# First layer of a two-layer decoder step: back rotation inside the output matmul, gelu as one ScalarE function, features kept in (channel, group) order

## The chip, the cores and the metric

The kernel runs on one core of a Trainium2 chip. The metric is the device time of one execution in microseconds (us); lower is better. A core has a matrix engine (PE, with its weight loads shown apart as PEld), a vector engine (DVE), an activation engine (ACT), a general engine (POOL) and a queue engine (SP) that issues the DMA transfers. Each engine works through its own instructions in the order in which they stand; between engines they wait on semaphores.

## The reference, cut to what matters

The model is one step of a decoder trunk: one S5 state-space layer, then one stick-breaking attention layer with a shared K/V. Only the S5 layer is touched. Cut to that:

```python
def _s5_layer(x, h0, ...):                    # x: 1024 prompt rows and 8 x 8 sample rows, 1024 features
    h = _rms_norm(x, g_pre)
    u, z = split(h @ w_in)                    # 1024 columns each
    y, hr, hi = _s5_scan(u, h0, ...)          # 64 groups of 16 channels, 64 complex states each
    y = jax.nn.gelu(y)                        # the tanh form
    y = y * jax.nn.sigmoid(y @ w_glu + b_glu) # the gate
    y = y * jax.nn.silu(z)
    return x + _rms_norm(y @ w_out, g_post), hr, hi

# _s5_scan, for each group: bu = w * (B u);  h[t] = lam * h[t-1] + bu[t]  (complex);
# y = Re(C h) + d_skip * u;  the last h is an output
```

## The kernel before, in words

**Stages.** The kernel norms the input rows and turns them to [feature, token] (`xh`, `xl`: every float32 operand is split into two parts, and a product takes three one-pass matmuls, lines 147 to 149). Then comes the S5 layer's main loop (`for ft in range(KT)`, eight tiles of 128 features, 8 groups of 16 channels each), then the gate (`s5_glu`), the output projection (`s5_out`) and the attention. Tokens are kept as 8 steps of a chunk by W = 136 columns (128 prompt chunks, then 8 samples).

**The projections.** `gemm_u(ft)` and `gemm_z(ft)` make one tile of u or z: three column blocks (408, 408 and 272 columns) times 8 k tiles times three matmuls, 72 in all. The u tile goes to DRAM (`u_d`), the z tile too (`zs_d`). In the loop `gemm_u(ft + 2)` and, from ft = 3, `gemm_z(ft - 3)` stand beside the S5 work; the last three z tiles are asked for after the loop. `weights` loads a tile of weights and splits it: ACT copies the high part (line 140), DVE or (odd z tiles) POOL subtracts to give the low part (line 141).

**The loop, tile's matrices.** For each ft: `wb`, `ep`, `fk`, `kp`, `cs` are built by DVE and POOL (all through the helper at line 205, so that they carry one line; they are told apart by tile name). `ep` is turned by PE (line 336) into `et`; `kp` (line 349) is moved by eight DMAs into the triangular matrix `tg` (line 360); `cs` is spread by four DMAs into `cf` = the cosines and sines (`cof`, `sif`; line 378).

**The loop, units.** The tile's u comes back from DRAM as `ug` with rows (step, channel) by eight DMAs (line 389). The 8 groups then go in three units of 3, 3 and 2 groups. A unit: PE makes the chunk inputs `pg` (line 394); ACT copies the two halves of `pg` crosswise into `tb` (400, 401); DVE and POOL rotate (`ta`, `tb`); DVE scans over the chunks (408); ACT copies the halves of the scanned states crosswise into `ts` (412, 413); POOL multiplies `ts` by the sines, DVE multiplies `ta` by the cosines and adds the two into `hs` (the back rotation), and into `l1` for the last state; PE adds two float32 products into one bank, `fk` with `hs` (425) and `tg` with `ug` (426); ACT evacuates to `yg` (427). After the three units comes gelu over the whole tile: ACT Square (430), DVE (431), ACT Sigmoid (432), DVE multiply. Eight DMAs write it to `y_d` (436).

**After the loop.** `yr` is loaded from `y_d` (452) and split by ACT and DVE (453, 454); the gate's matmuls read it.

**What sets the order.** The order on each engine is made by a scheduler that walks the program by modelled times and priorities: the two blocks under `tc.high_priority(OFA)` are put ahead of the projections, which fill PE between them. A pool with `bufs=n` hands out n buffers under a tag; the n+1st waits for the first's readers.

The lines that the steps below rest on most:

```python
tt(Q, ts[:, :n], ts[:, :n], sif[:, gl], ALU.mult)
tt(V, ta[:, :n], ta[:, :n], cof[:, gl], ALU.mult)
tt(V, hs[:, :n, 1:NC], ta[:, :n, 0 : NC - 1], ts[:, :n, 0 : NC - 1], ALU.add)
tt(V, l1[:, gsl], ta[:, :n, NC - 1], ts[:, :n, NC - 1], ALU.add)
```

(`V` is DVE, `Q` is POOL.) The functions in full, with the line numbers of the profile:

## Time and profile before

| what | value |
|---|---|
| median of 3 runs | 1519.7 us (1519.53 to 1520.04) |
| span of the profiled execution, first to last instruction | 1514.9 us |
| PE busy over the span | 1425.9 us, 94% |
| DVE busy over the span | 967.0 us, 64% |
| ACT busy, POOL busy | 733.8 us, 516.4 us |
| S5 loop with PE's and DVE's share, 105 to 325 us | PE 189.25 of 220 us, DVE 196.88 of 220 us |
| gate, 359 to 442 us | PE 83.00 of 83 us |

The span is 4.8 us below the median of the timed runs; what lies around it is outside the first and the last instruction. Busy time of PE counts pipelined matmuls by modelled ends; in a dense stretch the distance between the starts of two matmuls is their price. "PEclk" is the clock that TensorE was granted, as a share of full speed. An idle time is named with what ended it. The stretch that the change touches lies between 75 and 360 us.

### The profile page before, as it was taken

To read this page: it belongs to the slowest core of one execution; us is meant where nothing else is said; L and a number is where in the kernel's file an instruction comes from. 1 tells how busy PE (TensorE), PEld (TensorE's weight loads), DVE (VectorE), ACT (ScalarE), POOL (GpSimd) and SP (SyncE) were. 2 spreads that over 40 slices of the span, in tenths; PEclk is the share of its full clock that TensorE was granted. 3 is DMA by queue.
4 is the path that set the end of the run, shared out by engine and by line. 5 is a ranking of instruction groups with operands and counts; after the bars stand their busy time and mean duration, and the time that the engine had idled before them with its cause. 6 is when DMAs were issued, how large, how long until landed. Compare 5 with 4: busy or idle time off the path is not lost.

```text
span 1514.9 us, 26931 instructions
## 1 busy us (share of the span) xinstructions
PE 1425.9 (94%) x9648; PEld 1150.4 (76%) x9648; DVE 967.0 (64%) x1535; ACT 733.8 (48%) x1423; POOL 516.4 (34%) x497
## 2 busy tenths in 40 slices
PE   5978888889999989999999999999998999998997
PEld 4968788788986879999988877666565666564766
DVE  6788999857764641110022239897888797889635
ACT  6235454554443433333233337676766666576321
POOL 5565765633421123222211003333333232424200
PEclk9989999999999989999999999999999999999999
DMA  5344755575223343233288673979888786754026
GB/s 193 119 113 114 169 127 131 124 205 208 72 83 112 112 178 139 84 120 107 87 283 288 251 264 113 356 272 324 297 286 277 275 282 233 269 203 138 11 78 214
DMA packets 129415, 276.88 MB, mean 183 GB/s; under 512 B 21505, under 2 KB 66306, under 8 KB 129282
## 3 DMA queue, kind: packets, MB, share of 16 engines
q1 hardware_dynamic: 129282, 275.16, 55.1%
q8 instruction: 76, 1.25, 0.3%
q14 instruction: 57, 0.47, 0.1%
HBM read 225.01 MB, written 39.35 MB: 175 GB/s over the span
## 4 chain that ended last, share of the span: by engine, by line
PE 71%; DVE 12%; issue 4%; DMA 3%; POOL 3%; SPq 2%; ACT 2%; DVEq 0%; POOLq 0%; ACTq 0%
PE psmm L147 6%; PE psmm L149 6%; PE psmm L148 6%; PE psqk L147 6%; PE psqk L148 6%; PE psqk L149 6%; PE psa L946 5%; PE psb L1179 4%; PE psa L987 4%; PE psb L1161 4%; PE psqk L1136 3%; PE psqk L1137 2%; PE psa L147 2%; PE psa L149 2%; PE psa L148 2%
## 5 line engine op out<-in xcount | busy, mean ns | idle before, releaser
L1117 POOL TENSOR_TENSOR ql<-q,qh 128x256 fp32r<-128x256 f32 x64 | 60.9, 952 | 282.2 <-ACT qh L1116 235.4
L1138 ACT ACTIVATE F<-psqk,bp 128x384 f32<-128x384 f32 (+2 forms) x192 | 111.4, 580 | 64.2 <-PE psqk L1137 50.7
L1143 DVE TENSOR_TENSOR_SCAN F<-F,maskb 128x256 f32<-128x256 f32 (+3 forms) x128 | 131.6, 1033 | 13.3 <-ACT F L1138 12.8
L1146 POOL TENSOR_TENSOR S<-S,F 128x255 f32<-128x255 f32 (+3 forms) x64 | 100.8, 1574 | 114.7 <-DVE F L1145 26.5
L1139 ACT ACTIVATE S<-psqk,bp 128x384 f32<-128x384 f32 (+2 forms) x192 | 111.4, 583 | 21.0 <-PE psb L1161 20.9
L1161 PE MATMUL psb<-cst,S 128*128 128x128 f32 x576 | 95.9, 283 | 4.8 <-DVE og L1183 3.8
L1161 PEld LDWEIGHTS psb<-cst,S 128*128 128x128 f32 x576 | 66.6, 142 | 35.6 <-issue 20.1
L1145 DVE TENSOR_TENSOR_SCAN F<-F 128x384 f32<-128x384 f32 (+1 forms) x64 | 79.0, 1234 | 20.1 <-ACT F L1138 19.5
L1179 PE MATMUL psb<-at,vr 128*64 128x256 f32 (+1 forms) x640 | 89.0, 367 | 1.2 <-DVE at L1165 1.2
L946 PE MATMUL psa<-vp,sat 128*32 128x256 f32 x1024 | 86.1, 388 | 0.0
L1136 PE MATMUL psqk<-ks,qh 128*128 128x384 f32 (+2 forms) x192 | 77.2, 402 | 7.0 <-DVE ks L1101 5.2
L987 PE MATMUL psa<-kp,qbd 128*32 128x256 f32 x1024 | 75.5, 389 | 0.3 <-PE psb L1161 0.3
L1179 PEld LDWEIGHTS psb<-at,vr 128*64 128x64 f32 x640 | 46.5, 136 | 36.2 <-issue 10.4
L1165 DVE TENSOR_TENSOR at<-psb,maskb 128x384 f32<-128x384 f32 (+3 forms) x128 | 60.2, 477 | 20.5 <-PE psb L1161 19.9
L147 PE MATMUL psmm<-xh,whi_z 128*128 128x408 f32 (+1 forms) x192 | 65.7, 342 | 4.0 <-ACT ut L275 3.2
L147 PE MATMUL psmm<-x,whi_g 128*128 128x408 f32 (+1 forms) x192 | 66.6, 347 | 1.2 <-DVE gt L736 1.2
L147 PE MATMUL psmm<-xh,whi_u 128*128 128x408 f32 (+1 forms) x192 | 65.9, 343 | 0.2 <-ACT xh L253 0.2
L940 DVE TENSOR_TENSOR_SCAN sF<-sF 128x513 f32<-128x513 f32 x32 | 42.9, 1341 | 36.1 <-ACT sF L937 35.9
L1137 PE MATMUL psqk<-ks,ql 128*128 128x384 f32 (+2 forms) x192 | 65.4, 343 | 0.0
L1136 PEld LDWEIGHTS psqk<-ks,qh 128*128 128x128 f32 x192 | 36.8, 192 | 37.6 <-ACT S L1139 12.6
L148 PE MATMUL psmm<-xl,whi_u 128*128 128x408 f32 (+1 forms) x192 | 65.4, 340 | 0.0
L149 PE MATMUL psmm<-xh,wlo_u 128*128 128x408 f32 (+1 forms) x192 | 65.2, 339 | 0.0
(451 smaller groups left out, 4326.4 us busy)
## 6 DMA issues: line engine op xcount, KB each, us to landing
kp<-cache_kT SPq DMA_DIRECT2D x128, 512.0 KB, 5.8
vp<-cache_v SPq DMA_DIRECT2D x128, 512.0 KB, 5.3
cf<-cs SPq DMA_DIRECT2D x32, 256.0 KB, 4.1
q<-q_d SPq DMA_DIRECT2D x128, 64.0 KB, 4.1
u_d<-ut SPq DMA_DIRECT2D x8, 544.0 KB, 2.8
ug<-u_d SPq DMA_DIRECT2D x64, 68.0 KB, 3.1
y_d<-gt SPq DMA_DIRECT2D x64, 68.0 KB, 2.2
zs_d<-zt SPq DMA_DIRECT2D x8, 544.0 KB, 4.5
```

The lines of the kernel that those rows point to most:

```text
L147: nc.tensor.matmul(ps, sh, mh, start=(k == 0), stop=False)
L148: nc.tensor.matmul(ps, sh, ml, start=False, stop=False)
L149: nc.tensor.matmul(ps, sl, mh, start=False, stop=(k == n - 1))
L946: self.nc.tensor.matmul(po[32 * r : 32 * r + 32, 0:256], a[:, 32 * r : 32 * r + 32], rhs[:, r * 256 : (r + 1) * 256], start=start, stop=stop)
L987: nc.tensor.matmul(ps[32 * r : 32 * r + 32, half * 256 : half * 256 + 256], self.qbd[:, 2 * r + e, s, :], kt[:, :, 2 * r + e, :], start=(e ...
L1136: nc.tensor.matmul(ps[:, :m], qh[:, w], ks[:, c0 : c0 + m], start=True, stop=False)
L1138: nc.scalar.activation(F[:, c0 : c0 + m], ps[:, :m], AF.Sigmoid, bias=bp[:, 1, h : h + 1], scale=-0.125)
L1139: nc.scalar.activation(S[:, c0 : c0 + m], ps[:, :m], AF.Sigmoid, bias=bp[:, 0, h : h + 1], scale=0.125)
L1143: V.tensor_tensor_scan(fr, fr, self.maskb[:, 512 - m : 512][:, ::-1], 1.0, ALU.mult, ALU.max)
L1146: (Q if i % 2 else V).tensor_tensor(S[:, 0 : n - 1], S[:, 0 : n - 1], F[:, 1:n], op=ALU.mult)
L1161: nc.tensor.transpose(ps[:, j * 128 : (j + 1) * 128], S[:, (j0 + j) * 128 : (j0 + j + 1) * 128], self.ident)
L1179: nc.tensor.matmul(po[hs, o:256], self.vr[pi][:, j, hs], ats[hh][j // 4][:, j % 4, o:256], start=(j == 0), stop=(j == nj - 1))
```

## The change

It does these things, all in the S5 layer:

- The back rotation is no longer added up on DVE: DVE writes `ta * cos` straight into `hs`, POOL writes `ta * sin` into `tb`, and PE applies both to the output with two products, `fk` with `hs` and a new matrix `fs` (the halves of `fk` exchanged, one negated, by two ACT copies a tile) with `tb`. So three float32 matmuls a group in place of two; the two ACT copies into `ts` are gone. The `tg` product stands first.
- The last states are collected in `last` by small ACT copies, and rotated once after the loop.
- gelu is one ACT function (`Gelu_apprx_tanh`) that reads PSUM, once a unit; `yg`, Square, Sigmoid and the two DVE instructions are gone. Each unit's result is stored by itself.
- The channels of a u, z and y tile are kept in (channel, group) order: the weight columns are permuted while they are split (`by_channel`: the raw tile is read with a step of 16 elements), and the rows of `w_glu`, `b_glu` and `w_out` are permuted as they are loaded. `u_d` and `y_d` are laid out as [step, channel, group, column]: u is written in pieces of 136 columns and `ug` read by one DMA instead of eight; y is written by three DMAs a tile instead of eight and `yr` read in pieces of 136 columns.
- `dsk` (the skip term) has a tile of its own, and POOL masks it. `cf` is laid out by group.
- `weights` runs at a higher priority.

```diff
+def by_channel(ap):
+    return ap.rearrange("p k (g c) -> p k c g", c=GC)
 def split_w(nc, pool, raw, tag, shape, eng=None, bufs=2):
-    nc.scalar.activation(hi, raw, AF.Copy)
-    (eng or nc.vector).tensor_tensor(lo, raw, hi, op=ALU.subtract)
+    h, l = hi, lo
+    if len(raw.shape) > len(shape):
+        h, l = (x.rearrange("p k (c g) -> p k c g", c=GC) for x in (hi, lo))
+    nc.scalar.activation(h, raw, AF.Copy)
+    (eng or nc.vector).tensor_tensor(l, raw, h, op=ALU.subtract)
...
-        u_d = dram.tile([KT, 128, NTOK], F32, name="u_d")
-        y_d = dram.tile([KT, 128, NTOK], F32, name="y_d")
+        u_d = dram.tile([KT, L, GC, 8, W], F32, name="u_d")
+        y_d = dram.tile([KT, L, GC, 8, W], F32, name="y_d")
...
-                tt(V, sb[:16, 4], sb[:16, 4], bc(ident[:16, 0:16], 1, 8), ALU.mult)
+                tt(Q, dsk, dsk, bc(ident[:16, 0:16], 1, 8), ALU.mult)
...
+                fs = tp.tile([128, 8, L, GC], F32, name=f"fs{ft}", tag="fs")
+                nc.scalar.activation(fs[0:64], fk[64:128, :, 1:, :], AF.Copy)
+                nc.scalar.activation(fs[64:128], fk[0:64, :, 1:, :], AF.Copy, scale=-1.0)
...
-                for t in range(L):
-                    nc.sync.dma_start(ug[t * GC : (t + 1) * GC], usrc[t])
+                nc.sync.dma_start(ug, u_d[ft].rearrange("t c g n -> (t c) g n"))
...
-                    nc.scalar.activation(ts[0:64, :n], ta[64:128, :n], AF.Copy, scale=-1.0)
-                    nc.scalar.activation(ts[64:128, :n], ta[0:64, :n], AF.Copy)
+                    nc.scalar.activation(last[:, 0, gsl], ta[:, :n, NC - 1], AF.Copy)
-                    tt(Q, ts[:, :n], ts[:, :n], sif[:, gl], ALU.mult)
-                    tt(V, ta[:, :n], ta[:, :n], cof[:, gl], ALU.mult)
-                    tt(V, hs[:, :n, 1:NC], ta[:, :n, 0 : NC - 1], ts[:, :n, 0 : NC - 1], ALU.add)
-                    tt(V, l1[:, gsl], ta[:, :n, NC - 1], ts[:, :n, NC - 1], ALU.add)
+                    tt(Q, tb[:, :n, 0 : NC - 1], ta[:, :n, 0 : NC - 1], sif[:, gl, 0 : NC - 1], ALU.mult)
+                    tt(V, hs[:, :n, 1:NC], ta[:, :n, 0 : NC - 1], cof[:, gl, 0 : NC - 1], ALU.mult)
-                        nc.tensor.matmul(o, fk[:, g, 1:, :]..., hs[:, i, :], start=True, stop=False)
-                        nc.tensor.matmul(o, tg[:, g, :], ug[:, g, :], start=False, stop=True)
-                    nc.scalar.activation(yg[:, g0 : g0 + n, :], py..., AF.Copy)
+                        nc.tensor.matmul(py[:, o : o + W], tg[:, g, :], ug[:, g, :], start=True, stop=False)
+                        nc.tensor.matmul(py[:, o + 1 : o + W], fk[:, g, 1:, :]..., hs[:, i, 1:], start=False, stop=False)
+                        nc.tensor.matmul(py[:, o + 1 : o + NC], fs[:, g]..., tb[:, i, 0 : NC - 1], start=False, stop=True)
+                    nc.scalar.activation(gt[:, :n], py..., AF.Gelu_apprx_tanh)
+                    nc.sync.dma_start(ydst[:, gl], gt[:, :n])
-                nc.scalar.activation(gt, yg, AF.Square, scale=math.sqrt(0.044715))
-                V.scalar_tensor_tensor(gt, gt, 1.0, yg, op0=ALU.add, op1=ALU.mult)
-                nc.scalar.activation(gt, gt, AF.Sigmoid, scale=2.0 * math.sqrt(2.0 / math.pi))
-                tt(V, gt, gt, yg, ALU.mult)
-                for t in range(L):
-                    nc.sync.dma_start(ydst[t], gt[t * GC : (t + 1) * GC])
```

The order of the instructions moves with it. Two places matter below. The first is DVE around one unit of the loop (names: `ta` the rotated inputs and states, `tb` and `ts` their other halves, `l` the last states, `psb` the bank of line 394). Before:

```order
L205 TENSOR_TENSOR ta_0_1494<-ta_0_1494,cf_1389 128x384
L205 TENSOR_TENSOR ep_1958<-pk,wb_1949 128x1024
L205 TENSOR_TENSOR ta_3_1525<-psb_1521,cf_1389 128x384
L205 TENSOR_TENSOR sst<-psb_1521,pk 128x24
L205 TENSOR_TENSOR hs_775<-ta_0_1494,ts_0_1505 128x3x127
L205 TENSOR_TENSOR l_783<-ta_0_1494,ts_0_1505 128x3
L205 TENSOR_TENSOR ep_1958<-ep_1958,tm_1959 128x1024
L205 TENSOR_TENSOR ta_3_1525<-ta_3_1525,tb_3_1526 128x384
```

The same place in the changed kernel:

```order
L214 TENSOR_TENSOR ta_0_1465<-ta_0_1465,tb_0_1466 128x384
L214 TENSOR_TENSOR fk_1583<-pk,sb_1552 128x1152
L424 SCALAR_TENSOR_TENSOR ta_0_1465<-rho,ta_0_1465 128x128 x3
L214 TENSOR_TENSOR fk_1583<-fk_1583,tn_1584 128x1152
L214 TENSOR_TENSOR hs_775<-ta_0_1465,cf_1367 128x3x127
L214 TENSOR_TENSOR cs_1614<-cs_1614,m_1616 128x4x128
L214 TENSOR_TENSOR ta_3_1497<-psb_1493,cf_1367 128x384
L214 TENSOR_TENSOR sst<-psb_1493,pk 128x24
```

The sum into `hs` and the one into `l` are gone; `hs` now follows its scans and stands ahead of the next unit's first rotation, which before was put between the product and the sum. The second place is PE at the end of the loop: the last unit's products, and what stands behind them. Before:

```order
L425 MATMUL psa_3085<-hs_777,fk_2955 128x136
L426 MATMUL psa_3085<-ug_2997,tg_780 128x136
L147 MATMUL psmm_3374<-xh_90,whi_z_3343 128x408
L148 MATMUL psmm_3374<-xl_93,whi_z_3343 128x408
L149 MATMUL psmm_3374<-xh_90,wlo_z_3344 128x408
```

And in the changed kernel:

```order
L437 MATMUL psa_2991<-ug_2911,tg_779 128x136
L438 MATMUL psa_2991<-hs_776,fk_2865 128x135
L441 MATMUL psa_2991<-tb_6_2981,fs_2870 128x127
L156 MATMUL psmm_3011<-xl_92,whi_z_3006 128x408
L157 MATMUL psmm_3011<-xh_89,wlo_z_3007 128x408
L155 MATMUL psmm_3011<-xh_89,whi_z_3006 128x408
```

Before, 108 matmuls of z (one and a half tiles) stand between the last unit's products and the first matmul of the gate; in the changed kernel it is 287 (four tiles, but for one matmul). PE changes between the projections and the loop's float32 work 75 times before and 111 times after, counted from the first transposes of line 336 to the gate.

## Rows read from the trace of the kernel before

**Rows 1.** Windows: stretch, length, busy us (instructions) by engine, PEclk, DMA share, GB/s.

```profile
core 0: us, PE busy (x) PEld busy (x) DVE busy (x) ACT busy (x) POOL busy (x), PEclk, DMA share, GB/s
105.00:325.00 220.00, 189.25 (x1214) 174.73 (x1215) 196.88 (x305) 110.02 (x214) 138.40 (x109) 0.95 0.56 135
325.00:359.00 34.00, 30.56 (x185) 29.61 (x185) 18.06 (x13) 16.96 (x21) 5.99 (x2) 1.00 0.87 294
359.00:442.00 83.00, 83.00 (x504) 82.97 (x503) 63.95 (x59) 35.88 (x64) 38.33 (x16) 1.00 0.20 66
```

**Rows 2.** Waits, 105 to 325 us: engine, line, what ended it, total us, times, longest.

```profile
PE psa L425 <- DVE hs L205: 8.7, 9, 2.0
PE psb L394 <- DVE sst L205: 8.2, 4, 4.6
```

**Rows 3.** Groups by shape, 105 to 325 us: busy us, mean ns, idle before.

```profile
L205 DVE TENSOR_TENSOR hs<-ta,ts 128x381 f32<-128x381 f32 x15 | 15.7, 1049 | 1.2 <-POOL ts L205 1.1
L205 DVE TENSOR_TENSOR hs<-ta,ts 128x254 f32<-128x254 f32 x8 | 8.3, 1040 | 0.8 <-POOL ts L205 0.8
L205 DVE TENSOR_TENSOR l<-ta,ts 128x3 f32<-128x3 f32 x16 | 10.8, 673 | 0.0
L205 DVE TENSOR_TENSOR l<-ta,ts 128x2 f32<-128x2 f32 x8 | 5.6, 706 | 0.0
L431 DVE SCALAR_TENSOR_TENSOR gt<-gt,yg 128x1088 f32<-128x1088 f32 x7 | 9.7, 1391 | 0.0
L205 DVE TENSOR_TENSOR gt<-gt,yg 128x1088 f32<-128x1088 f32 x7 | 9.1, 1302 | 0.0
L205 DVE TENSOR_TENSOR sb<-sb,cst 16x128 f32<-16x128 f32 x6 | 3.3, 544 | 0.0
```

**Rows 4.** By tile, 105 to 325 us: count, shortest/median/longest ns, first and last start.

```profile
L205 DVE TENSOR_TENSOR hs<-ta,ts x23: 410/844/2717, 114.9 to 323.7; 128x381 f32<-128x381 f32 x15, 128x254 f32<-128x254 f32 x8
L205 DVE TENSOR_TENSOR l<-ta,ts x24: 144/156/2322, 104.8 to 324.0; 128x3 f32<-128x3 f32 x16, 128x2 f32<-128x2 f32 x8
L431 DVE SCALAR_TENSOR_TENSOR gt<-gt,yg x7: 1275/1279/1631, 134.2 to 311.4; 128x1088 f32<-128x1088 f32 x7
L205 POOL TENSOR_TENSOR tm<-pk,wb x6: 2858/3133/4922, 113.5 to 264.9; 128x1024 f32<-128x1024 f32 x6
```

**Rows 5.** Timeline of PE: start us, length us, group.

```profile
292.46 0.39 PE L426 MATMUL psa<-ug,tg 128*128 128x136 f32 x2
292.69 0.40 PE L425 MATMUL psa<-hs,fk 128*128 128x136 f32 x2
294.48 0.46 PE L149 MATMUL psmm<-xh,wlo_z 128*128 128x408 f32 x1
294.77 0.35 PE L147 MATMUL psmm<-xh,whi_z 128*128 128x408 f32 x1
```

**Rows 6.** Timeline of PE in z tiles, 12 and 16 matmuls apart, and the gate's first.

```profile
336.69 0.35 PE L147 MATMUL psmm<-xh,whi_z 128*128 128x408 f32 x1
338.91 0.34 PE L147 MATMUL psmm<-xh,whi_z 128*128 128x408 f32 x1
...
288.72 0.29 PE L148 MATMUL psmm<-xl,whi_z 128*128 128x272 f32 x1
290.74 0.29 PE L149 MATMUL psmm<-xh,wlo_z 128*128 128x272 f32 x1
...
342.49 0.35 PE L147 MATMUL psmm<-yh,whi_g 128*128 128x408 f32 x1
```

**Rows 7.** Windows, the gate's weights alone: busy us of PE, PEld, DVE, ACT.

```profile
342.49:359.00 16.51, 12.57 (x49) 8.62 (x50) 1.22 (x1) 1.04 (x1) 1.00 0.87 318
```

**Rows 8.** Groups by shape: attention's output written with a step; evacuation and split without.

```profile
L665 ACT ACTIVATE qt<-psqk 128x384 f32<-128x384 f32 x8 | 7.5, 940 | 30.0 <-PE psqk L149 30.0
L275 ACT ACTIVATE ut<-psmm 128x408 f32<-128x408 f32 x16 | 8.1, 509 | 23.7 <-PE psmm L149 17.5 <-issue 6.1
L141 DVE TENSOR_TENSOR wlo_z<-wraw_z,whi_z 128x1024 fp32r<-128x1024 f32 x4 | 4.8, 1208 | 0.0
```

More of the change, by code (lines that the diff above doesn't have):

```diff
@@ L215, in weights @@
         def weights(which, ft):
-            wraw = wp.tile([128, KT, 128], F32, name=f"wraw_{which}{ft}", tag="wraw", bufs=1)
-            nc.sync.dma_start(wraw, io["a_win"][ft + (KT if which == "z" else 0)])
-            return split_w(nc, wp, wraw, f"{which}{ft}", [128, KT, 128], Q if which == "z" and ft % 2 else V)
+            with tc.high_priority(2 * OFA):
+                wraw = wp.tile([128, KT, 128], F32, name=f"wraw_{which}{ft}", tag="wraw", bufs=1)
+                nc.sync.dma_start(wraw, io["a_win"][ft + (KT if which == "z" else 0)])
+                return split_w(nc, wp, by_channel(wraw), f"{which}{ft}", [128, KT, 128], Q if which == "z" and ft % 2 else V)
         gpre = start.tile([128, D], F32, name="gpre")
@@ L296, in s5_layer @@
             hs = tp.tile([128, 3, W], F32, name=f"hs{i}")
-            Q.memset(hs, 0.0)
             h_t.append(hs)
+        last = par.tile([128, 4, G], F32, name="last")
         tgs = [tp.tile([128, 8, 128], F32, name=f"tg{i}") for i in range(2)]
@@ L386, in s5_layer @@
                 ug = work.tile([128, 8, W], F32, name=f"ug{ft}", tag="ug")
-                usrc = u_d[ft].rearrange("(g c) (t n) -> t c g n", c=GC, t=L)
-                for t in range(L):
-                    nc.sync.dma_start(ug[t * GC : (t + 1) * GC], usrc[t])
-                yg = work.tile([128, 8, W], F32, name=f"yg{ft}", tag="yg", bufs=1)
+                nc.sync.dma_start(ug, u_d[ft].rearrange("t c g n -> (t c) g n"))
+                ydst = y_d[ft].rearrange("t c g n -> (t c) g n")
                 for g0, n in ((0, 3), (3, 3), (6, 2)):
@@ L439, in s5_layer @@
         nc.sync.dma_start(gains, io["b_gains"])
+        nc.scalar.activation(last[0:64, 1], last[64:128, 0], AF.Copy, scale=-1.0)
+        nc.scalar.activation(last[64:128, 1], last[0:64, 0], AF.Copy)
+        tt(V, last[:, 2:4], last[:, 0:2], last[:, 2:4], ALU.mult)
+        tt(V, l1, last[:, 2], last[:, 3], ALU.add)
         nc.sync.dma_start(io["o_sp"], l1)
```

54 lines of the change are left out of this document (29 added, 25 removed).

## The prediction, made before the changed kernel ran

> **What bounds the kernel now.** I read the windows first, by stage. In the gate PE is busy 83.00 of 83 us, so whatever ends earlier ahead of it moves the end by as much. In the loop, from 105 us (first output product) to 325 (last), PE is busy 189.25 of 220 us at a clock of 0.95, and DVE 196.88 of 220: PE waits for 30.8 us there, and the engine that has no time left is DVE [rows 1]. Then the waits: the two longest of PE are both ended by DVE, on `hs` (the state that the output product reads) and on `sst`, which stands behind the first rotation of a unit [rows 2]. Then the DVE groups and their spread: `hs` takes 410 ns at the shortest and 2717 at the longest, the tiny `l` 144 and 2322 [rows 3, 4]. So part of DVE's busy time is waiting inside an instruction. From 325 to 359 PE has 3.4 us idle, in the change from z to the gate [rows 1].
>
> I sum against the profiled span of 1514.9 us; the median of the timed runs, 1519.7, is 4.8 above, and I carry a difference over to it unchanged.
>
> **The frame.** Let X be the loop's length in the changed kernel, from its first output product, which I leave at 105 us (the tiles' matrices and the u projections ahead of it are the same). The order puts 287 z matmuls, four tiles, behind the loop, where before it was 108. In a dense stretch 408 columns cost (338.91 - 336.69)/12 = 0.185 us and 272 columns (290.74 - 288.72)/16 = 0.126 [rows 6], so a tile is 48 x 0.185 + 24 x 0.126 = 11.9 us and four are 47.6. The gate then starts at 105 + X + 47.6. Before, 12.6 us of gate work was done by 359 us [rows 7], so it began, as if unbroken, at 346.4. The span changes by X - 193.8. The loop must fall from 220 to 194 us to break even, since 30.3 us of z (47.6 - (342.49 - 325.2) [rows 6]) leave it for behind it.
>
> **What PE gets and loses.** Added: 64 float32 matmuls (`fs` with `tb`, one a group) at 0.23 us, the distance from one product to the next (292.69 - 292.46): 14.7 us. Its neighbour of 136 columns gives the price; 127 columns would be 0.215 at the least, 13.8. Changes between projection and float32 work rise by 36; across one the step was 0.29 in place of 0.185 us (294.77 - 294.48), so 36 x 0.1 = 3.6 us [rows 5]. The loop's PE work now, at full clock, is 189.25 - 0.05 x 220 = 178.2 us. Floor for X: 178.2 + 14.7 + 3.6 - 30.3 = 166.2.
>
> **What DVE loses and gets.** Inside the loop the change takes away the `hs` sums, the `l` sums, two passes of gelu a tile and the `sb` mask: 15.7 + 8.3 + 10.8 + 5.6 + 9.7 + 9.1 + 3.3 = 62.5 us as they ran [rows 3]. Unhindered they are 23 x about 0.5 (`hs` from 410 ns), 24 x 0.15, 7 x 1.275 and 7 x 1.26 [rows 4], with 6 masks at 0.27, taken as half of their mean: some 34 us. The difference, 28 us, is blocked time that another instruction may inherit. The product into `hs` replaces the one into `ta` at the same size and is no term. Added: the low parts of the weights read the raw tile with a step. No row reads so; the nearest is attention's evacuation, which writes with a step of 8 elements: 940 ns for 384 columns against 509 for 408 without, about twice a column [rows 8]. Between nothing and twice, I take twice: six splits on DVE in the loop at +1.2 us (1208 ns now) are +7. So DVE holds 196.9 - 62.5 + 7 = 141 us to 196.9 - 34 + 7 = 170 us. At the share it is busy now (0.895), X is 158 to 190.
>
> **The other engines.** ACT is busy half the loop [rows 1]. Out go the two copies into `ts`, the plain evacuation, Square and Sigmoid; in come gelu from PSUM in the evacuation's place, two copies a tile into `fs`, small copies and splits of twice the price. That about cancels, and it ends no wait of PE worth naming. One more load of an activation table falls into the z tail, under 47.6 us of PE work. POOL keeps its two products a unit, gets the mask (8 small instructions) and slower splits of the odd z tiles: 138 us of 220 become some 145. The new wait is on `fs`: one buffer, so ACT's copies wait for the previous tile's last product, and behind them on ACT stand the evacuations and the copies into `tb`. Two copies of 1024 columns are about 2.5 us by the evacuation's rate [rows 8], once a tile, with z and u matmuls on PE meanwhile: between nothing and 8 x 2.5 = 20 us. I take little, since PE has some 20 projection matmuls (3.7 us) between the tiles' products. SP issues eleven transfers fewer a tile. The pieces of 136 columns that u and y now go through are those in which `ug` and `y_d` moved before; u has a tile of slack and y has the z tail, so I cost the new layout at nothing; uncovered, a slow `yr` would cost its landing, about 5 us.
>
> **A rule to weigh.** `hs` stretches from 410 to 2717 ns and POOL's `tm` from 2858 to 4922 [rows 4]: the two engines hold each other up. The Trainium skill, SBUF — State Buffer, section "SBUF: two separate sides", says that a DVE instruction with two SBUF inputs and a POOL instruction that reads SBUF exclude each other for a whole instruction. By that every removed sum would also free POOL; but as a strict lock it does not fit, since DVE and POOL were busy 335 us in 220 [rows 1], and most of DVE's busy time is of this sort. As far as it holds, it makes a rival (below, "blocked").
>
> **The forecast.** DVE's range (158 to 190) and PE's floor (166) lie close together, so neither engine alone sets X: each will wait for the other at times. PE now loses 42 us to waits and clock over 220. I take X = 183: DVE near its upper end, because POOL's work, which blocks it, stays, and PE with 17 us of waits and slow clock left. That gives 183 - 193.8 = -10.8 us, so 1519.7 - 10.8 = 1508.9, call it 1509. Behind the loop nothing is late: `yr`, the split into `yh` and `yl` and the first `yv` have 47.6 us of z on PE, so the 3.4 us of idle go too (they are in the 346.4).
>
> **The rivals.**
> - *PE is dense.* The blocked time goes with the removed instructions, DVE has slack, and PE runs at its floor with few waits: X = 166 to 175, -28 to -19 us, 1492 to 1501. For it: DVE's lower end is below the floor. Against: the change adds waits of PE on two engines, DVE and POOL, for each group.
> - *Blocked: POOL paces the loop.* The slower side. A unit is a chain: ACT's crosswise copies, POOL's product, DVE's sum and scans, POOL's second product, PE. POOL runs in order, and `tm` (2.9 to 4.9 us) and its like stand between. If the 28 us of blocked time only change their victim and POOL's waits stretch with them, X stays at 197 to 210: +3 to +16 us, 1523 to 1536. It decides from X = 194 on, and only because four z tiles were moved behind the loop: the loop may be 10% faster and the kernel slower. For it: POOL's work does not shrink. Against: POOL is idle for 82 us of the loop.
> - *The step is dear.* If reading with a step costs DVE three times, not twice, six splits in the loop cost 14.5 us rather than 7, and in the gate eight more add 19 us to DVE's 63.95 of 83 [rows 1]: it would be full, and PE would wait. 1517 to 1525. The Trainium skill, SBUF — State Buffer, section "Door 1: The DMA port swizzle", says that accesses beyond a 16-byte line pay a penalty, without a price for DVE; by the row of twice the gate's DVE is at 74 of 83 and hides it.
> - *No gain as described* (gelu slower than the copy that it replaces, a transfer that blocks): 1520 and above. Nothing in the rows speaks for it.
>
> **How the numbers follow.** Forecast 0.42 (1502 to 1516), dense 0.22, blocked 0.20, dear step 0.11, no gain 0.05. A difference under 0.2% (3 us) cannot be told from none here. Faster by more: the forecast's case but for its upper edge, and the dense one: 0.63. Within: the edges of the forecast, of "blocked" and of "dear": 0.13. Slower: the rest, 0.24. The range leaves out the densest end and the worst of "blocked": 1495 to 1528; the forecast's own is 1502 to 1516.
>
> **What would show it.** In the profile after: last output product at about 105 + 183 = 288 us (below 275: dense; above 299: slower than before); DVE busy 141 to 170 us in the loop; no idle of PE between the z tail and the gate; one output product every 0.23 us; the low-part splits at 1.2 us (no price), 2.4 (mine) or 3.6 (dear); gelu from PSUM at about 509 ns for 408 columns. I am wrong if PE's waits move to `tb` from POOL or to `fs` from ACT with totals above 20 us, or if the gate's PE is not full.

## The result and the profile after: 1.1% slower

| | before | changed |
|---|---|---|
| median (lowest to highest) | 1519.9 us (1519.5 to 1523.6) | 1537.2 us (1536.6 to 1539.3) |
| ratio to before, 95% interval | | 1.0109 [1.0094, 1.0123] |
| span of the profiled execution | 1514.9 us | 1534.0 us |
| first matmul of the gate, and from it to the end | 342.5 us (345.9 as if unbroken), 1169.0 us | 365.6 us, 1168.4 us |

The forecast was 1509 us, in a range from 1495 to 1528: the sign is wrong and the time is outside. Counted from the gate's first matmul (before: as if unbroken, since PE waited for 3.4 us in the gate's first 17) the two kernels take the same time within 0.6 us, so the 19.1 us of the span are lost ahead of it.

Windows of the changed kernel: start and end, length, then busy us (instructions) of PE, PEld, DVE, ACT and POOL, the granted clock, the DMA share and GB/s. The stretches are the first 50 us, the loop from its first to its last output product, from there to the gate, the gate's first 84 us, and all up to the gate.

```profile
0.00:50.00 50.00, 29.59 (x160) 27.06 (x161) 34.85 (x85) 28.50 (x49) 22.31 (x74) 1.00 0.43 147
107.45:316.99 209.54, 171.52 (x1183) 159.51 (x1182) 169.85 (x244) 96.19 (x192) 130.63 (x115) 0.95 0.48 127
316.99:365.63 48.64, 47.77 (x289) 47.34 (x288) 18.92 (x11) 22.89 (x27) 10.87 (x4) 1.00 0.81 252
365.63:450.00 84.37, 84.37 (x513) 84.35 (x512) 50.78 (x48) 37.69 (x56) 31.42 (x12) 1.00 0.25 71
0.00:365.63 365.63, 298.51 (x1929) 282.20 (x1930) 268.77 (x426) 167.16 (x297) 202.45 (x232) 0.96 0.51 147
```

The same of the kernel before, for the first 50 us, the loop (again from first to last output product, a little other than in [rows 1]) and all up to the gate:

```profile
0.00:50.00 50.00, 32.62 (x175) 30.07 (x176) 35.60 (x94) 26.35 (x50) 22.30 (x75) 1.00 0.50 169
105.38:325.45 220.07, 189.32 (x1215) 174.90 (x1216) 196.50 (x305) 110.02 (x214) 138.02 (x109) 0.95 0.56 135
0.00:342.49 342.49, 286.72 (x1801) 268.42 (x1801) 284.72 (x490) 162.09 (x305) 202.33 (x225) 0.96 0.55 145
```

The loop is 209.5 us long, 10.5 less than before. But 48.6 us of work stand behind it in place of 17.0, and it begins 2 us later. 194 us were needed to break even. DVE did lose work (169.9 busy of 209.5 in place of 196.5 of 220), and PE did not get it: PE has 38.0 us without work in the loop, before 30.8.

The loop is not one stage. The changed kernel's loop in three parts by DVE's work (its first seven tiles, its wait for the eighth, the eighth), and then the first 176 us of the loop before:

```profile
107.45:281.00 173.55, 136.43 (x948) 124.67 (x947) 158.11 (x221) 80.18 (x164) 120.68 (x105) 0.94 0.50 128
281.00:298.76 17.76, 16.86 (x112) 16.62 (x111) 0.00 (x1) 7.52 (x13) 3.83 (x4) 0.98 0.50 141
298.76:316.99 18.23, 18.23 (x128) 18.22 (x127) 11.74 (x23) 8.48 (x16) 6.12 (x7) 1.00 0.27 99
```

```profile
105.38:281.00 175.62, 148.95 (x952) 136.72 (x953) 162.38 (x245) 86.37 (x169) 117.13 (x91) 0.94 0.57 137
```

PE loses 37.1 of its 38.0 us in the first seven tiles. There DVE is busy 0.91 of the time, hardly less than before (0.92). Behind them DVE has nothing to do for 17.8 us, in which PE finishes the last u tile and works at z.

Waits of PE in the loop (line, what ended it, us in all, times, longest), to be held against [rows 2]:

```profile
PE psa L438 <- DVE hs L214: 20.9, 11, 3.2
PE psm L351 <- DVE ep L214: 5.7, 4, 2.1
PE psb L410 <- DVE sst L214: 4.2, 2, 2.6
PE psa L441 <- POOL tb L214: 1.4, 1, 1.4
```

The wait on `hs` has grown from 8.7 to 20.9 us, though `hs` now takes one DVE instruction less. Where DVE's time went is seen in single instructions, by tile: count, shortest/median/longest ns, first and last start (all of the changed kernel, 103 to 318 us). They answer to [rows 4].

```profile
L214 DVE TENSOR_TENSOR ta<-ta,tb x24: 407/685/3210, 104.7 to 311.9; 128x384 f32<-128x384 f32 x16, 128x256 f32<-128x256 f32 x8
L214 DVE TENSOR_TENSOR ta<-psb,cf x23: 410/543/557, 102.7 to 311.1; 128x384 f32<-128x384 f32 x15, 128x256 f32<-128x256 f32 x8
```

The sum `ta<-ta,tb` was not touched by the change. Its groups in the loop by shape, of the changed kernel and then of the one before (busy us, mean ns of one, idle before it):

```profile
L214 DVE TENSOR_TENSOR ta<-ta,tb 128x384 f32<-128x384 f32 x15 | 21.5, 1435 | 6.1 <-POOL tb L214 6.1
```

```profile
L205 DVE TENSOR_TENSOR ta<-ta,tb 128x384 f32<-128x384 f32 x15 | 10.4, 693 | 0.0
```

Its mean has doubled: it has inherited blocked time that `hs` and `l` had [rows 3, 4]. The product of the same size that reads PSUM on one side is never over 557 ns.

What such an instruction waits for can be seen in the order of time: start us, length us, first on DVE, then on POOL.

```profile
145.76 1.21 DVE L214 TENSOR_TENSOR ep<-pk,wb 128x1024 f32<-128x1024 f32 x1
146.89 2.17 DVE L214 TENSOR_TENSOR ta<-ta,tb 128x256 f32<-128x256 f32 x1
```

```profile
145.91 2.87 POOL L214 TENSOR_TENSOR tm<-pk,wb 128x1024 f32<-128x1024 f32 x1 [0.23 <-DVE wb L214]
```

The sum needs 407 ns where nothing holds it up. Here it begins beside POOL's `tm`, which ends at 148.78, and itself ends 0.28 us later. All 42 DVE instructions of this loop that took over 0.4 us longer than the shortest of their shape have two inputs in SBUF and began while a POOL instruction ran; the time that each took beyond that shortest one is the time to the end of a POOL instruction (that one, or one close behind it), less 0.10 to 0.23 us. Together these excesses are 49.0 us; counted in the same way they are 51.9 us in the loop before (53 instructions). This is called blocked time below. It also stands in POOL's times: `tm` begins 0.15 us after DVE's `ep` and outlasts it by 1.8 us, while the larger product `tn` (128x1152) with no DVE instruction beside it took 2.16 us (at 85.8 us).

Groups up to 480 us: line, engine, what is written from what, shapes and count, busy us and mean ns of one, idle before. They answer to [rows 8]:

```profile
L148 ACT ACTIVATE whi_u<-wraw_u 128x1024 fp32r<-128x1024 f32 x8 | 15.9, 1992 | 7.2 <-PE psmm L156 4.8 <-DMA wraw_u<-a_win 2.4
L149 DVE TENSOR_TENSOR wlo_u<-wraw_u,whi_u 128x1024 fp32r<-128x1024 f32 x8 | 17.8, 2228 | 8.4 <-ACT whi_u L148 8.4
L149 DVE TENSOR_TENSOR wlo_g<-wraw_g,whi_g 128x1024 fp32r<-128x1024 f32 x8 | 15.8, 1977 | 22.9 <-ACT whi_g L148 22.8
L149 POOL TENSOR_TENSOR wlo_z<-wraw_z,whi_z 128x1024 fp32r<-128x1024 f32 x4 | 11.9, 2970 | 4.7 <-ACT whi_z L148 3.4 <-DMA y_d<-gt 1.2
L445 ACT ACTIVATE gt<-psa 128x408 f32<-128x408 f32 x16 | 8.0, 502 | 6.5 <-PE psa L441 5.9 <-DMA u_d<-ut 0.5
```

Reading with a step of 16 elements costs DVE 1977 ns in the gate against 1224 in the kernel before, and ACT 1992 against 1052. The mean of 2228 for `wlo_u` holds blocked time: the shortest took 1883 ns and the longest 3547, before 1195 and 2979. gelu from PSUM takes 502 ns, as long as the plain evacuation did (509).

### The profile page after: what moved, and what is told of

Read it like the earlier page. It is cut to its first block, busy times and chain, and to the rows that moved or that the text cites. A ratio compares the mean times of both kernels' runs of the same rounds, so it can differ in the third digit from the quotient of the medians.

```text
span 1534.0 us, 26976 instructions
## 1 busy us (share of the span) xinstructions
PE 1436.3 (94%) x9776; PEld 1163.3 (76%) x9776; DVE 943.3 (61%) x1465; ACT 739.1 (48%) x1410; POOL 513.6 (33%) x503
## 4 chain that ended last, share of the span: by engine, by line
PE 65%; DVE 12%; issue 9%; POOL 7%; DMA 4%; ACT 2%; SPq 1%; DVEq 0%; POOLq 0%; ACTq 0%
PE psmm L155 5%; PE psmm L157 5%; PE psmm L156 5%; PE psa L960 5%; PE psqk L155 4%; PE psqk L156 4%; PE psqk L157 4%; PE psb L1193 4%; PE psa L1001 4%; PE psb L1175 4%; PE psqk L1150 3%; DMA cf<-cs 2%; DVE ta L214 2%; PE psqk L1151 2%; PE psa L157 2%
## 5 line engine op out<-in xcount | busy, mean ns | idle before, releaser
L1157 DVE TENSOR_TENSOR_SCAN F<-F,maskb 128x256 f32<-128x256 f32 (+3 forms) x128 | 131.3, 1031 | 13.6 <-ACT F L1152 13.1
L1175 PEld LDWEIGHTS psb<-cst,S 128*128 128x128 f32 x576 | 66.4, 142 | 35.6 <-issue 20.5
L1159 DVE TENSOR_TENSOR_SCAN F<-F 128x384 f32<-128x384 f32 (+1 forms) x64 | 79.0, 1234 | 20.3 <-ACT F L1152 19.7
L1193 PEld LDWEIGHTS psb<-at,vr 128*64 128x64 f32 x640 | 46.6, 136 | 36.1 <-issue 10.5
```

Source lines behind the costliest of these rows:

```text
L1157: V.tensor_tensor_scan(fr, fr, self.maskb[:, 512 - m : 512][:, ::-1], 1.0, ALU.mult, ALU.max)
L1175: nc.tensor.transpose(ps[:, j * 128 : (j + 1) * 128], S[:, (j0 + j) * 128 : (j0 + j + 1) * 128], self.ident)
L1193: nc.tensor.matmul(po[hs, o:256], self.vr[pi][:, j, hs], ats[hh][j // 4][:, j % 4, o:256], start=(j == 0), stop=(j == nj - 1))
```

## The experiments

Each ratio is to runs of the kernel before on the same chip; their medians lay between 1519.0 and 1520.2 us. Intervals are about 0.2% to either side, so two kernels less than some 4 us apart are not told apart.

**First question: which part of the change costs?** Theory A: the added PE work is paid in full. Rivals: the step (S), and after the first four runs the priority of the weights (Q) and the layout itself (T).

*Without the step* (after, `e1`; the same for `w_glu`):

```diff
-                return split_w(nc, wp, by_channel(wraw), f"{which}{ft}", [128, KT, 128], Q if which == "z" and ft % 2 else V)
+                return split_w(nc, wp, wraw, f"{which}{ft}", [128, KT, 128], Q if which == "z" and ft % 2 else V)
...
-    a["a_win"] = cols(i["a_w_in"][0])
+    a["a_win"] = mixed(i["a_w_in"][0])
...
```

> The changed kernel, with the columns of w_in and w_glu packed in (channel, group) order ahead of the launch, so that the splits read without a step. Theory A (paid in full): PE waits in the loop for the length of a unit's chain, not for DVE's throughput, so the 64 added products (14.7 us by the prediction) come out at the end nearly whole and the step costs only where it stands on the path, in the first weights: 1531 to 1537 us, loop of some 200 us. Rival S (the step): ACT's splits at 2.0 us in place of 1.05 and DVE's at 2.0 to 2.5 in place of 1.2 hold up the copies into tb and the scans; without the step the loop falls under 194 us and the time to 1515 to 1525.

*Back rotation summed on DVE again* (after, `e2`; `fs` and `last` go, `ts` and `l` come back as in the kernel before):

```diff
-                        nc.tensor.matmul(
-                            py[:, o + 1 : o + NC], fs[:, g].rearrange("p a b -> p (a b)"), tb[:, i, 0 : NC - 1], start=False, stop=True
-                        )
...
+                    tt(V, hs[:, :n, 1:NC], ta[:, :n, 0 : NC - 1], ts[:, :n, 0 : NC - 1], ALU.add)
+                    tt(V, l1[:, gsl], ta[:, :n, NC - 1], ts[:, :n, NC - 1], ALU.add)
```

> The changed kernel with the back rotation summed on DVE again (ts, hs and l as before; fk and tg only on PE, no fs, no last), gelu and layout as changed. Theory A (paid in full): PE is rid of 64 products and gets no more idle, so 12 to 15 us come back: 1522 to 1525 us. Rival S (the step): DVE is filled by the dear splits and gets the sums on top (34 to 40 us more), so the loop grows: 1540 us or more. Rival P (POOL paces): POOL's two products a unit are the same in both, so the time hardly moves by DVE, and the answer lies near A.

*Gelu alone* (before, `e3`):

```diff
-                    nc.scalar.activation(yg[:, g0 : g0 + n, :], py[:, : n * W].rearrange("p (a b) -> p a b", a=n), AF.Copy)
+                    nc.scalar.activation(gt[:, g0 : g0 + n, :], py[:, : n * W].rearrange("p (a b) -> p a b", a=n), AF.Gelu_apprx_tanh)
```

> The kernel before, with nothing changed but gelu: one function from PSUM in the evacuation's place, gt in two buffers; the stores stay eight a tile, the rotation and the layout as before. DVE loses 16 passes of about 1.3 us (20 us in the loop), ACT 16 of 1.1. Theory A (paid in full, DVE's throughput does not bound): PE's idle hardly falls, but the chain at the end of the loop is shorter by the gelu passes: 1513 to 1519 us. Rival (DVE bounds the loop, as the prediction had it): 20 us less on an engine that is 0.9 busy bring the loop from 220 to 198 to 205: 1500 to 1508 us.

*Gelu and rotation in the old layout* (`e6`: the edit of `e3`, and the rotation's part of the change, with one buffer of `gt`).

> The kernel before with gelu as one function and the back rotation on PE (fs, last, three products a group), but the old layout: no step in the splits, eight DMAs for ug and y, no priority of the weights; one buffer of gt. Theory A (paid in full): the products are paid as in the changed kernel, 1528 to 1536 us, and 10 to 15 us above the one with gelu alone. Rival S (the step and the layout are what costs): below the kernel before, 1505 to 1515 us.

*The priority taken away*, in the changed kernel (`e7`), without the step (`e8`), and without step and third product (`e9`); `e5` is `e9` with the priority.

```diff
-            with tc.high_priority(2 * OFA):
```

> The changed kernel with the weights' loads and splits at their old priority, all else as changed. Theory Q (priority): the splits, now ahead of the rows' own norm at the start and ahead of the units in the loop, hold up the chain; without it 3 us come back ahead of 50 us (PE busy there 32.6 us as before, not 29.6) and some more in the loop: 1528 to 1533 us. Rival T (the layout itself: the pieces of 136 columns, the coefficients by group): the start comes back, 3 us, and no more: 1534 to 1537 us.

> The changed kernel without the step in the splits (columns packed ahead of the launch) and without the priority: what is left of the change is gelu, the rotation on PE and the layout of u, y and the coefficients. Theory Q (priority): as gelu and rotation in the old layout, 1523 to 1527 us. Rival T (the layout itself costs): as with the step alone undone, 1529 to 1531 us. If step and priority were only hurtful together: near 1526 us too, and the runs with one of them each tell.

> As the run before it, and with the back rotation summed on DVE again: gelu as one function and the new layout, without step and priority. Theory Q (priority): as gelu alone, 1511 to 1516 us, perhaps less, since ug comes by one transfer instead of eight. Rival T (the layout itself costs): 1525 us or more.

> The two-product kernel in the new layout and with the priority, without the step. The step's price with two products is the difference to 1535.3 us with it. If the step costs as much as with three products (7 us): 1527 to 1530 us; if DVE, fuller here, makes it dearer: under 1525 us; if it is nothing here: 1533 to 1536 us.

| kernel | products a group | layout, step, priority | median us | ratio to before |
|---|---|---|---|---|
| e3 | 2 | old | 1513.1 | 0.9954 [0.9937, 0.9971] |
| e9 | 2 | new, no step, no priority | 1520.7 | 1.0006 [0.9996, 1.0015] |
| e5 | 2 | new, no step, priority | 1524.7 | 1.0038 [1.0027, 1.0049] |
| e2 | 2 | new, step, priority | 1535.3 | 1.0100 [1.0078, 1.0122] |
| e6 | 3 | old | 1525.9 | 1.0052 [1.0035, 1.0069] |
| e8 | 3 | new, no step, no priority | 1528.7 | 1.0059 [1.0035, 1.0083] |
| e1 | 3 | new, no step, priority | 1530.2 | 1.0075 [1.0056, 1.0093] |
| e7 | 3 | new, step, no priority | 1532.5 | 1.0084 [1.0064, 1.0104] |
| changed | 3 | new, step, priority | 1537.2 | 1.0109 [1.0094, 1.0123] |

gelu alone gains some 6 us. Everything else loses. The rotation on PE costs 12.8 us in the old layout (`e6` - `e3`, which also differ in the buffers of `gt` and in the place of the `tg` product) and 1.8 where the kernel is already late (changed - `e2`). The step costs 3.8 to 10.6 us (`e7` - `e8`, changed - `e1`, `e2` - `e5`), the priority 1.5 to 4.7 (`e1` - `e8`, `e5` - `e9`, changed - `e7`), the layout itself 2.8 to 7.6 (`e8` - `e6`, `e9` - `e3`); the smallest of these are within the error. Along the path gelu, rotation, layout, priority, step the differences are -6, +12.8, +2.8, +1.5 and +7.0. That they come to about the whole (+18.1, by the ratio +17) shows nothing, since each begins where the last one ended; by another path the same parts have other sizes. Of the expectations, A's held for `e3`, and within 2 us for `e6` and `e1`; its 1522 to 1525 for `e2` missed by ten, and S by five the other way (P's time that hardly moves came, though P put it near A's). S fell in `e1` and `e6`, and the rival for `e3`. Q's time for `e7` held, but not its reason: PE had 29.9 us of work in the first 50 us there too, so the step alone delays the start as well (30.4 with the priority alone in `e1`, 31.2 with neither in `e8`). `e8` and `e9` came out between Q and T: priority and layout both cost. `e5` says that the step is dearest where DVE is fullest. Why the layout costs what is left was not settled. `e9` lets PE wait 9.7 us for gelu to free a bank ahead of the `tg` product, which led to the run with `tg` first (`e13`, below); that did not confirm it.

**Second question: is it PE's added work?** Theory A against a loop that is set by something else.

*Third product left out (`e10`), or read from `hs` (`e11`)*, both on `e6`; the edit of `e11`:

```diff
-                            py[:, o + 1 : o + NC], fs[:, g].rearrange("p a b -> p (a b)"), tb[:, i, 0 : NC - 1], start=False, stop=True
+                            py[:, o + 1 : o + NC], fs[:, g].rearrange("p a b -> p (a b)"), hs[:, i, 1:NC], start=False, stop=True
```

> Gelu and rotation in the old layout (1525.9 us), with the third product (fs with tb) left out; everything else stays, POOL's product into tb and ACT's copies into fs too. The output lacks the half of the rotated state that this product adds. Theory A (its PE time is paid in full): 14.7 us of products and some switches go, the time falls by 14 to 20 us, to 1506 to 1512 us, below gelu alone (1513.1), since DVE's sums are gone as well. Rival W (hidden in waits): PE's idle takes up what the products leave, and the time stays above 1518 us.

> Gelu and rotation in the old layout (1525.9 us), where the third product reads hs in place of tb: the same work on PE, but no wait for POOL's second product, whose result nobody reads (the output is then another sum). Theory A (the work is paid): 1523 to 1527 us, within 3 us of the same kernel with tb. Rival P (POOL paces the units by tb): the wait goes and the loop with it, 1512 to 1519 us.

Measured: 1535.1 us (1.0105 [1.0078, 1.0132]) without the product, nine *more* than with it; 1530.5 (1.0077 [1.0051, 1.0104]) with `hs` for `tb`. Theory A misses in both, by 23 us and by 3: 128 matmul instructions fewer (two to a product), and nothing is gained; W named the side, though not that it would be slower. Rival P, the wait for `tb`, falls with it. The windows of `e6` and then of `e10`, the loop and from its end to the gate:

```profile
109.42:309.67 200.25, 175.46 (x1167) 160.87 (x1168) 152.56 (x242) 89.42 (x191) 133.29 (x108) 0.94 0.58 135
309.67:354.95 45.28, 45.28 (x277) 45.26 (x276) 14.00 (x11) 19.53 (x25) 7.48 (x4) 1.00 0.78 270
```

```profile
109.46:311.51 202.05, 158.01 (x1009) 145.33 (x1009) 163.06 (x242) 87.23 (x189) 128.63 (x107) 0.88 0.58 134
311.51:361.55 50.04, 50.04 (x308) 50.01 (x308) 15.70 (x11) 20.69 (x27) 9.84 (x4) 1.00 0.71 243
```

With 17 us less PE work in it the loop is as long (202.1 and 200.3 us), and the scheduler, which takes the shorter loop for granted, leaves 308 matmuls behind it in place of 277. But the order on the other engines is another too: the same 242 instructions of DVE take 163.1 us in place of 152.6, and the blocked time in them is 50.7 us in place of 35.5. So in this pair less work on PE does not shorten the loop; what the product itself costs can't be read from it.

*z moved into the loop* (`e6` with `with tc.high_priority(600):` around `gemm_z(ft - 3)`; `e14` is the same on `e3`), and *`tg` first* (`e3` with its two products exchanged, `e13`):

```diff
-                gemm_z(ft - 3)
+                with tc.high_priority(600):
+                    gemm_z(ft - 3)
```

> Gelu and rotation in the old layout (1525.9 us, 276 z matmuls behind the last output product), with the z tiles at the loop's own priority: 150 stand behind it. Theory A (work plus idle ahead of the gate counts, not where z stands): z is only moved; the loop grows by about what the tail loses (126 matmuls, 21 us), and the time stays within 4 us, 1522 to 1530 us. Rival Z (z behind the loop is what loses: in the loop it would have filled PE's waits): 1508 to 1518 us.

> Gelu alone in the old kernel (1513.1 us; 174 z matmuls behind the last output product), with the z tiles at the loop's priority: 110 stand behind it. If z fills waits of PE in a loop that a chain sets: the loop stays at 208 us and the tail falls by 64 matmuls, 10 us: 1503 to 1508 us. If PE's fixed order only moves the waits, as with rotation on PE: 1510 to 1516 us.

> Gelu alone in the old kernel (1513.1 us), with the two products of a group exchanged: tg with ug opens the bank, fk with hs follows, as in the changed kernel. Theory L (order): PE now takes a bank of the output before hs is there and waits for its evacuation, as in the run with the new layout and two products, where PE waited 9.7 us for gelu ahead of the tg product: 1517 to 1522 us, and most of what the layout seemed to cost is this. Rival (harmless): 1511 to 1515 us, and the layout itself costs.

Measured: 1526.8 us (1.0047 [1.0033, 1.0061]) against 1525.9, and 1513.5 (0.9960 [0.9947, 0.9972]) against 1513.1. Moving z to and fro changes nothing in the time, as A had it: in `e12` the loop grows from 200.3 to 219.1 us while the tail falls from 45.3 to 24.5. Theory L falls, `tg` first is harmless: 1510.6 us (0.9935 [0.9913, 0.9957]).

**Third question: what makes the loop 200 us long?** Theory C: DVE and POOL hold each other up. Rivals: two units in flight (B), and the transfers of the coefficients (D), which take 22 us in the changed kernel's chain of waits.

*POOL's four products of the tile's matrices left out* (on the changed kernel; the same for `tm2` and both `m`):

```diff
-                tt(Q, tm, bc(liv, 3, GC), bc(wb[:, 1], 2, L), ALU.mult)
-                tt(V, ep, ep, tm, ALU.subtract)
+                tt(V, ep, ep, ep, ALU.subtract)
```

> The changed kernel without POOL's four products a tile for the tile's matrices (tm, tn and the two m, some 62 of its 131 us in the loop); DVE's instructions behind them stay, with their own tile as both inputs, so ep, fk and cs hold other numbers. The loop from first to last output product lasted 200 to 213 us in every kernel run so far with z behind it, though DVE's busy time in it went from 153 to 183 us and PE's from 158 to 181. Theory C (the chain between DVE and POOL sets the loop): it falls under 185 us, DVE's instructions come back to their short times (ta with tb 690 ns, not 1380), and the time to 1505 to 1520 us. Rival D (coefficients' transfers and queues set it): still above 198 us, 1530 us or more.

*Three buffers for `tb` and `hs`; no transfer of the coefficients* (each on the changed kernel):

```diff
-                    tb = work.tile([128, 3, NC], F32, name=f"tb{ft}_{g0}", tag="tb")
+                    tb = work.tile([128, 3, NC], F32, name=f"tb{ft}_{g0}", tag="tb", bufs=3)
...
-                    hs = h_t[units % 2]
+                    hs = h_t[units % 3]
...
```

> The changed kernel with three buffers instead of two for tb and hs (gt has two in place of three): the third product lets a unit hold its tb until PE has read it. Rival B (two units in flight set the loop): it falls under 195 us, 1520 to 1528 us. Theory C (DVE and POOL hold each other up, whatever is in flight): 200 us or more, 1533 to 1545 us; the scheduler puts 308 z matmuls behind the loop in place of 287, some 3 us more.

```diff
-                        nc.sync.dma_start(cf[64 * h : 64 * h + 64, 4 * i : 4 * i + 4].rearrange("p g e c -> p (g e c)"), cs[64 * i : 64 * i + 64].rearrange("p g e a b -> p (g e a b)"))
...
+                cf = cs.rearrange("p g e a b -> p g e (a b)")
...
```

> The changed kernel without the four transfers a tile that spread the coefficients: the units read cs where it is made (three buffers), with the wrong groups' numbers; DVE's and POOL's work is the same. In the chain of waits of the changed kernel, cf takes 22 us of the loop, the longest share after DVE's. Rival D (these transfers set the loop): under 190 us, 1515 to 1522 us. Theory C: 198 us or more, 1530 us or more.

Measured: `e16` 1536.9 us and `e17` 1537.1, no other than the changed kernel, with loops of 207.8 and 208.9 us: B and D fall. `e15` takes 1510.8 us (0.9941 [0.9921, 0.9962]), 26 less, as C had it (its loop misses C's 185 us by one). Its windows, the loop, the tail and all up to the gate:

```profile
103.67:289.96 186.29, 167.26 (x1185) 161.51 (x1184) 132.96 (x234) 95.58 (x188) 82.44 (x88) 0.94 0.52 138
289.96:338.51 48.55, 47.88 (x289) 47.28 (x288) 18.95 (x11) 22.86 (x27) 10.87 (x4) 1.00 0.82 253
0.00:338.51 338.51, 292.99 (x1929) 282.99 (x1930) 233.16 (x426) 168.62 (x297) 140.62 (x200) 0.96 0.56 159
```

The tail has the same 289 matmuls; the loop is 23 us shorter. Up to the gate DVE runs 426 instructions in both kernels, in 233.2 us here and in 268.8 in the changed one: 35.6 us of DVE's busy time went with POOL's four products. The run can't say how much of the gain came by shorter DVE instructions and how much by waits for POOL's results that went with them, and the second inputs of four DVE instructions were changed. The next pair leaves nothing out.

*The four products on DVE instead of POOL* (`e18` on the changed kernel, `e19` on `e13`):

```diff
-                tt(Q, tm, bc(liv, 3, GC), bc(wb[:, 1], 2, L), ALU.mult)
+                tt(V, tm, bc(liv, 3, GC), bc(wb[:, 1], 2, L), ALU.mult)
...
-                tt(Q, m1, uas, ubs, ALU.mult)
+                tt(V, m1, uas, ubs, ALU.mult)
```

> The changed kernel with the four products a tile for the tile's matrices (tm, tn, both m) on DVE instead of POOL; the numbers are the same. DVE gets 32 instructions more, of about 1.2, 1.4 and two times 0.9 us a tile as their like last on DVE, 35 us in all; POOL loses 62. Theory C in the form that POOL's work lengthens DVE's instructions: without those products DVE's others were 37 us shorter, so DVE stands about even, the waits between the two are gone, and the loop falls to 195 to 205 us: 1520 to 1533 us. Rival V (DVE's own work is what counts): DVE is busy over 190 us in the loop, which grows: 1540 us or more.

> The fastest kernel so far, gelu as one function and tg first (1510.6 us), with the same four products a tile on DVE instead of POOL. DVE carries the sums of the back rotation here, 180 us busy of 208, so 35 us more find less room. Theory C: still a little faster or equal, 1503 to 1511 us. Rival V: 1515 us or more.

Measured: `e18` 1519.3 us, 18 less than the changed kernel (0.9999 [0.9989, 1.0009] to the kernel before), with a loop of 197.2 us; `e19` **1492.8 us, 0.9829 [0.9812, 0.9846]: the fastest of all, 1.7% under the kernel before**, and below what theory C gave. In `e18`, first the window up to the gate, then the sum by tile:

```profile
0.00:348.33 348.33, 296.82 (x1928) 283.13 (x1929) 267.65 (x458) 168.03 (x297) 155.64 (x200) 0.96 0.55 154
```

```profile
L214 DVE TENSOR_TENSOR ta<-ta,tb x24: 405/542/558, 104.1 to 299.8; 128x384 f32<-128x384 f32 x16, 128x256 f32<-128x256 f32 x8
```

The price of one such product in the loop, first on POOL (changed kernel), then on DVE (`e18`):

```profile
L214 POOL TENSOR_TENSOR tm<-pk,wb 128x1024 f32<-128x1024 f32 x6 | 17.3, 2880 | 4.3 <-DVE wb L214 4.3
```

```profile
L214 DVE TENSOR_TENSOR tm<-pk,wb 128x1024 f32<-128x1024 f32 x6 | 7.3, 1210 | 0.0
```

DVE does 32 instructions more (458 and 426) and is busy no longer (267.7 and 268.8 us): the others became shorter by as much as the new ones take. `ta<-ta,tb` is never over 558 ns now, where it went up to 3210. In the loop the blocked time falls from 49.0 to 25.0 us, and the idle time of DVE that POOL's results end from 11.3 to 3.2, so the shorter instructions are the larger part. What is left comes from POOL's two products a unit and its splits. Rival V, that DVE's own work counts, falls. Of the 2880 ns on POOL about one is waiting for DVE's `ep`, as shown above. In `e19` the loop and the tail are:

```profile
100.71:299.79 199.08, 178.54 (x1197) 166.97 (x1197) 173.71 (x321) 95.53 (x201) 96.42 (x85) 0.96 0.60 143
299.79:322.64 22.85, 22.85 (x140) 22.82 (x139) 10.27 (x8) 11.99 (x15) 4.34 (x2) 1.00 0.98 343
```

A loop of 199 us with PE at 179 busy, and 23 us behind it: the gate begins at 322.6 us. The 18 us come with the rotation on PE and without it. So the blocking is not what the change added; it held both kernels up, and kept the change from its gain. What the change added is in the table of the first question.

## Why the prediction was wrong, point by point

- **The frame held.** It made the gate's start 105 + X + 47.6. Measured: 107.5 + 209.5 + 48.6 = 365.6, and what comes behind changes by 0.6 us. (The 12.6 us of gate work in [rows 7] are the matmuls on the high part of the weights alone; with those on the low part they are 13.1, and the gate before began, as if unbroken, at 345.9 rather than 346.4. That is half a us.) The miss of 30 us in span is 26.5 in X (183 forecast), 2.5 in the start that was "left at 105", and 1 in the tail.
- **The step that failed** is "At the share it is busy now (0.895), X is 158 to 190", and with it the 17 us "of waits and slow clock left" for PE that make X 183. DVE's busy time came to 169.9 us, the top of the forecast range of 141 to 170, but in a loop of 209.5, a share of 0.81. The share was not a constant of the loop: DVE was busy 0.91 of the first seven tiles and not at all in the 17.8 us before the eighth, when PE was at u and z. PE's work in the loop was less than the floor of 166.2 us (161.0, reckoned as there), but 38.0 us without work and 10.5 of slow clock (0.05 of the loop), 48.5 in all, stood beside it in place of 17. From run to run the loop followed DVE's busy time only in part: 153 us of it (`e6`) went with a loop of 200 us, 183 (`e2`) with 213.
- **The term behind it** is the 28 us of blocked time that "another instruction may inherit", of which X took most but not all as staying. DVE's busy time without the blocked time fell by 24 us, about as forecast (34 off, 7 on); the blocked time fell from 51.9 to 49.0 us, so nearly all of it was inherited. That filled DVE in the first seven tiles, where PE waited for it.
- **The argument that let it fail** is the one against the lock: DVE and POOL were busy 335 us in 220, so they can't exclude each other. That counts as work what is partly waiting. An instruction that waits for its operands' access is busy in the profile, as the prediction itself had said of `hs`; two engines that block each other can both look busy. In the loop before, 51.9 us of DVE's busy time were such waiting, and `e15` took 35.6 us off DVE up to the gate. The sum with two SBUF inputs went from 407 to 3210 ns beside POOL's matrix products and to 558 without them, the product with one input in PSUM kept to 557, and every stretched instruction ended with POOL's (above). The Trainium skill, SBUF — State Buffer, section "SBUF: two separate sides", which was weighed and set aside, says that a DVE instruction with two SBUF inputs and a POOL instruction that reads SBUF take a shared port in turn, each for its whole length. These rows agree with it.
- **"Blocked" was the right rival in kind**, with its loop of 197 to 210 us, and had 0.20. Its time of 1523 to 1536 was still 1 to 14 us short, by the late start and the tail. What was put against it, that POOL is idle for 82 us, is no argument: most of POOL's idle time is waiting for DVE. Of 78.9 us in the changed kernel's loop the scans alone end 39.9 (24 waits of `tb<-ta,cf`), other DVE instructions 16.5.
- **PE's terms** were right in size: 0.22 to 0.23 us a product, PE's work up to the gate 298.5 against 286.7 us (forecast 18 more, 12 seen at a granted clock of 0.96 in both). Of the 19.7 us by which the gate begins later, as if unbroken, 12 are this work and 8 more idle time of PE (67.1 us in place of 59.2); the forecast had the work paid for by 29 us less idle. But taking the work out again did not bring the time back: in `e2` PE's work up to the gate is 286.7 us as before, its idle time is 76.9, and the gate begins at 363.6, only 2.1 us earlier; `e10` was slower. In the old layout it was otherwise: PE's work up to the gate is 305.2 us in `e6` and 285.0 in `e3`, the idle time 49.7 and 55.8, and the gate begins 14 us later. So what the product costs on the clock (1.8 to 12.8 us by the table) hangs on the kernel around it, and the runs do not settle it.
- **"The step is dear"**: forecast twice on DVE, measured 1.6 times (1977 against 1224 ns in the gate), and 1.9 on ACT. The term of 7 us of DVE time came to 5 (five splits in the loop, 11.1 us with blocked time in place of 6.0), but on the clock the step cost up to 10.6 us.
- **The start** was taken as unchanged. PE has 3.0 us less done by 50 us. The step and the priority both have part in it: ACT now begins the split of the second u tile's weights at 18.5 us, ahead of input rows, in place of 22.5, and is at it for 1.96 us in place of 1.05. With neither (`e8`) 1.4 us are still missing, and why is open.
- **Right:** gelu (502 ns, forecast 509; a gain of 6 us alone), `fs` (PE's reading of it held ACT up by 2.7 us in all), hardly any idle of PE between z and gate (0.9 us), a full gate (84.37 of 84.37 us), and a loop that got shorter while the kernel got slower, since four z tiles stand behind it. Of the signs named in advance the last output product came at 317 us, past the 299 of "slower than before"; waits moved to `tb` or `fs` did not come: the wait stayed on `hs`.

## What to carry to other kernels

Before dividing an engine's busy time by its share, look at the shortest and the longest time of one instruction with the same shape: where they are far apart, and the long ones end when an instruction of POOL ends, part of the busy time is blocking, and taking instructions away hands it to the next one. Divide by stage, too: an average share of 0.81 was 0.91 in one stretch and nothing in another. Then try moving POOL's work onto the blocked engine: here, for four products a tile, it gained 18 us in one kernel and as much in another, at no busy time. Where a scheduler fills an order by modelled times, judge a change by when the next stage starts, not by how long the loop is.

## What was not expected of the hardware

- A product of 128 x 1024 numbers from two SBUF tiles took 2880 ns on POOL, of which about one is waiting for DVE, and 1210 on DVE; one of 128 x 1152, unhindered, 2156 and 1448. While POOL did the four of a tile, DVE lost about as much in its other instructions (36 us up to the gate, `e15`) as the four take on DVE itself (9.7 + 11.6 + 16.8 = 38.1 us up to the gate in `e18`).
- Less PE work went with a lower clock: in `e10` the granted clock of the loop (a mean of its two levels, 1.2 and 2.4 GHz) was 0.88 with PE 44 us without work, in `e6` 0.94 with 25. That may be part of why the removed product gave nothing; the two runs can't say how much, and it is no rule: the changed kernel's loop had 0.95 with PE 38 us without work.
- The same step in reading costs each engine another factor: ACT 1052 to 1992 ns, DVE 1224 to 1977, POOL 2673 to 2970.
